# A two-layer mLSTM and RG-LRU trunk on one core: in-projections moved from channel-major to token-major

## The chip, the cores and the metric

The kernel runs on one core of a Trainium2 chip. The metric is the device time of one execution in microseconds. One execution was also taken with the hardware profiler; its trace gives the rows shown below. TensorE does the matmuls (PE, with its weight loads as PEld), VectorE is DVE, ScalarE is ACT, GpSimd is POOL, and SP only issues DMAs.

## The reference

The trunk takes x of 256 tokens by 2048 channels through two layers. All is float32. Cut to what matters, a layer is:

```python
u = rms_norm(x, norm_g)
p = u @ w_in                                    # 2048 x 12304
qk, v, o, z_a, ig, fg, xb, z_b = split(p)       # 2048 columns each, ig and fg 8 each
q, k = split(silu(causal_dwconv(qk, qk_conv)))  # 4 taps along the tokens
h = mlstm(q, k, v, i_pre, log_f) * sigmoid(o)   # 8 heads: q, k of 128, v of 256
y_a = head_norm(h) * head_norm_g * silu(z_a)
xc = causal_dwconv(xb, lru_conv_w) + lru_conv_b
y_b = rg_lru(xc, w_a, b_a, w_x, b_x, lam) * silu(z_b)   # gates: 8 blocks of 256x256
x = x + concat(y_a, y_b) @ w_out                # 4096 x 2048
```

After the second layer comes a last `rms_norm` with `final_g`.

## The kernel before

Each layer runs in four groups g of two heads, which is 512 columns of every part of `w_in`. A group's work is a list of items: the in-projection chunks `o`, `v`, `qk`, `xb`, `z`, `zb` of 512 columns each, the gate matmuls (`gate`), and four chunks of the out-projection of the group before (`out`, the fill). `_sequence` (L35) writes this order out by hand. In group 0 of a layer it is o, v, qk, xb, z, gate; in group 1 it is o, zb of group 0, v, qk, two fills, xb, two fills, z, gate, zb; later groups are the same without the zb of group 0. The last group of the first layer is followed by its out-projection in the order of units 0, 2, 1, 3; the last group of the second by `last_out` (L814), whose first eight halves need only `ya` and whose other eight need `yb`.

Weights come as units of 128 x 2048 floats (1 MB), loaded by SP into three buffers `raw` (L230) and used in two halves. `prepare` (L248) makes a half ready three halves ahead (`AHEAD`): ScalarE rounds it to `wH` (L261), VectorE subtracts to get the rest `wL` (L262, in the trace at the helper's L151). There are four buffers of each. Every product is taken in three parts (high by high, high by low, low by high), since the matmul's operand type holds fewer bits than float32.

Two matmul loops exist. `mm_a` (L266, token-major) holds 128 tokens of x as the stationary operand and streams 512 weight columns: for each of 16 row tiles and 2 token tiles three matmuls of 512 columns, 96 in a chunk; the result has tokens on the partitions. `mm_b` (L282, channel-major) holds 128 weight columns and streams tokens: for `wH` one matmul of 512 columns (high and low part of x side by side), for `wL` one of 256 columns, 128 matmuls in a chunk; the result has channels on the partitions. Before the change qk, xb and zb use `mm_b` in two parts `s_` of 256 channels, because the convolutions and the recurrence run along the tokens within a partition; o, v, z and the out-projection use `mm_a`.

A channel-major result is evacuated by `evac_b` (L363): a copy on ScalarE, an addition and a product on VectorE; the product with `rb` puts in the norm's factor for each token. For the convolutions it goes into a padded tile (`evac_pad`, L370), and `conv` (L353) takes one ScalarE operation and three VectorE operations for each tile of 128 channels.

What follows a chunk is a Python generator in a queue `bg`. After each half, `pump` (L202) lets the first generators in the queue emit instructions until a budget (`credit`) is used up: 1.05 for at most two generators, else 2.6. `require(key)` runs the first generators until something is there, for instance `xc` before the gate matmuls (`gate_before`) or `ybT` before the second unit of an out chunk. The engines' instruction streams come from a scheduler that orders instructions by readiness and by their place in the program.

Of the kernel before, what the change touches and what calls it, by code (L numbers as in the profile page):

```python
# [16 lines left out]
P = 128  # L17
# [10 lines left out]
AHEAD = 3  # L28

# [41 lines left out]

@with_exitstack
def tile_trunk(ctx, tc, x, xt, par, gw, gb, ws, final_g, out):
# [11 lines left out]
    st = {"nload": 0, "credit": 0.0, "pair": 0, "aux": 0}  # L85
# [42 lines left out]
    def load_x(c):  # L128
# [6 lines left out]
        nc.sync.dma_start(out=st["xa"][:, :, cs], in_=xv[:, :, cs])  # L135
        square_sum(c)
# [65 lines left out]
    def pump(budget):  # L202
        st["credit"] = min(st["credit"] + budget, budget)
        while bg and st["credit"] > 0:
            try:
                c = next(bg[0])
            except StopIteration:
                bg.popleft()
# [3 lines left out]
            st["credit"] -= c  # L212
# [16 lines left out]
    def load_unit(n, item, j):  # L229
        raw = wraw.tile([P, 2048], F32, tag="raw", name="raw")  # L230
        st["nload"] += 1
        u = blocks[item, j]
        if n < 4:
            w = 512 if n == 0 else 1024
            for o in range(0, 2048, w):
                if o % 1024 == 0:
                    load_xt(n, o // 1024)
                nc.sync.dma_start(out=raw[:, o : o + w], in_=ws[u][:, o : o + w])
        else:
            nc.sync.dma_start(out=raw, in_=ws[u])  # L240
        return raw

    def add_unit(mms, before=None, after=None):
        box = {}
        halves.append([dict(box=box, i=i, mm=mms[i], split=None,
                            before=before if i == 0 else None, after=after if i == 1 else None) for i in range(2)])

    def prepare(hf):  # L248
        n = len(xT_parts) if hf["i"] == 0 else 1
        if hf["i"] == 0:  # L250
            hf["box"]["raw"] = load_unit(n, *hf["at"])
            if n < 4:
                split_xT(0, n, xT_parts[n], range(4 * n, 4 * n + 4))
            if 4 <= st["nload"] < 8:
                load_x(st["nload"] - 4)
        r = hf["box"]["raw"][:, 1024 * hf["i"] : 1024 * hf["i"] + 1024]
        H = wsp.tile([P, 1024], F32R, tag="H", name="wH")
        L = wsp.tile([P, 1024], F32R, tag="L", name="wL")
        w = 1024 if n else 512
        for o in range(0, 1024, w):  # L260
            S.copy(out=H[:, o : o + w], in_=r[:, o : o + w])  # L261
            tt_(L[:, o : o + w], r[:, o : o + w], H.bitcast(F32)[:, o : o + w], ALU.subtract)  # L262
        hf["split"] = (H, L)


    def mm_a(acc, aH, aL, k0, first, last):  # L266
        def f(H, L):
            Hv = H.rearrange("p (k c) -> p k c", k=2)
            Lv = L.rearrange("p (k c) -> p k c", k=2)
            a_H, a_L, ps = aH(), aL(), acc()  # L270
            for k in range(2):
                kt = k0 + k
                for t in range(2):
# [3 lines left out]
                    PE.matmul(ps[:, t, :], a_H[:, kt, tsl], Hv[:, k, :], start=s, stop=False)  # L277
                    PE.matmul(ps[:, t, :], a_H[:, kt, tsl], Lv[:, k, :], start=False, stop=False)  # L278
                    PE.matmul(ps[:, t, :], a_L[:, kt, tsl], Hv[:, k, :], start=False, stop=e)  # L279
# [17 lines left out]
    def chunk_in(l, kind, g, postfn, beforefn=None):  # L297
# [9 lines left out]
        if kind in ("qk", "xb", "zb"):  # L307
# [5 lines left out]
        else:  # L313
            acc = make_acc()
            for u in range(4):
                mms = [mm_a(acc, lambda: st["x"][:, :, 0], lambda: st["x"][:, :, 1], 4 * u + 2 * i,
                            u == 0 and i == 0, u == 3 and i == 1) for i in range(2)]
                add_unit(mms, before=beforefn if u == 0 else None,
                         after=(lambda: postfn(acc())) if u == 3 else None)
# [33 lines left out]
    def conv(padt, o, ct, wcol, l, bias, oc=None):  # L353
        oc = ct if oc is None else oc
        wv = pars[:, l, wcol : wcol + 4]
        if bias is None:
            S.activation(out=o[:, oc, :], in_=padt[:, ct, 0:T], func=AF.Copy, scale=wv[:, 0:1])
        else:
            S.activation(out=o[:, oc, :], in_=padt[:, ct, 0:T], func=AF.Identity, scale=wv[:, 0:1], bias=bias)
        for j in range(1, 4):  # L360
            stt(o[:, oc, :], padt[:, ct, j : j + T], wv[:, j : j + 1], o[:, oc, :], ALU.mult, ALU.add)
# [7 lines left out]

    def evac_pad(l, acc):  # L370
        padt = work.tile([P, 2, 260], F32, tag="pad", name="padt", bufs=2)
        G.memset(padt[:, :, 0:3], 0.0)
        evac_b(l, padt[:, :, 3 : 3 + T], acc)
        return padt
# [112 lines left out]
    def v_post(l, g, acc):  # L487
# [11 lines left out]
        st["v", l, g] = (vH, vL)  # L499
        bg.append(e_gen(l, g))  # L500

    def qk_post(l, g, acc, h):
        padt = evac_pad(l, acc)

        def gen():
            qc = work.tile([P, 2, T], F32, tag="c4", name="qc", bufs=2)
            sg = work.tile([P, 2, T], F32, tag="sC", name="qsg")
            for ct in range(2):
                conv(padt, qc, ct, O_QKW + 4 * (8 * ct + 2 * g + h), l, None)
# [3 lines left out]
            yield 0.6  # L513
            q = work.tile([P, 2, 2, T], F32R, tag="xcs", name="qks")
            S.copy(out=q[:, :, 0, :], in_=qc)
            tt_(q[:, :, 1, :], qc, q.bitcast(F32)[:, :, 0, :], ALU.subtract)
            yield 0.6
            yield None
            yield None
            yield None  # L520
            yield None
            E, em, so, (vH, vL) = st["E", l, g], st["em", l], st["so", l, g], st["v", l, g]
            ps = aux("ps_S")
            for o_, ss_, ts__ in ((0, slice(0, 128), slice(0, 256)), (256, slice(128, 256), slice(128, 256))):
                mm3(ps[:, o_ : o_ + ts__.stop - ts__.start], q[:, 1, 0, ss_], q[:, 1, 1, ss_],
                    q[:, 0, 0, ts__], q[:, 0, 1, ts__])
            Pt = work.tile([P, 384], F32, tag="Pt", name="Pt")
            stt(Pt, ps[:, 0:384], DK_SCALE, E[:, h, :], ALU.mult, ALU.mult)
            PH = work.tile([P, 384], F32R, tag="sD", name="PH")
            PL = work.tile([P, 384], F32R, tag="sC", name="PL")  # L530
# [3 lines left out]
            yield None  # L534
            yield None
            yield None
            if h == 0:
                st["hh", l, g] = work.tile([P, 2, 2, 256], F32, tag="sE", name="hh")
                st["mv", l, g] = small.tile([P, 2, 2, 2], F32, tag="mv", name="mv", bufs=1)
            hh, mv = st["hh", l, g], st["mv", l, g]  # L540
            for t in range(2):
                pn = aux("ps_n")
                o = pn[:, 0:258]
                a = slice(P * t, P * t + P)
                mm3(o, PH[:, a], PL[:, a], vH[:, 0, h, :], vL[:, 0, h, :], last=t == 0)
                if t == 1:
                    mm3(o, PH[:, 256:384], PL[:, 256:384], vH[:, 1, h, :], vL[:, 1, h, :], first=False)
                dn = small.tile([P, 1], F32, tag="dn", name="dn")
                stt(dn, pn[:, 256:257], -1.0, em[:, t, 2 * g + h : 2 * g + h + 1], ALU.mult, ALU.max)
                tt_(dn, dn, pn[:, 256:257], ALU.max)  # L550
                V.reciprocal(out=dn, in_=dn)
                stt(hh[:, t, h, :], pn[:, 0:256], dn, so[:, t, 256 * h : 256 * h + 256], ALU.mult, ALU.mult)
                bs = small.tile([P, 6], F32, tag="bs", name="bs")
                V.bn_stats(out=bs, in_=hh[:, t, h, :])
                V.bn_aggr(out=mv[:, t, h, :], in_=bs)
                yield 1.1
            if h == 0:
                return
# [49 lines left out]
    def xb_post(l, g, acc, s_):  # L608
        padt = evac_pad(l, acc)

        def gen():
            if s_ == 0:
                st["xcf", l, g] = work.tile([P, 4, T], F32, tag="c4", name="xc", bufs=2)
                st["xcs", l, g] = work.tile([P, 4, 2, T], F32R, tag="xcs", name="xcs")
            xc, xs = st["xcf", l, g], st["xcs", l, g]
            for ct in range(2):
                tix = 4 * g + 2 * s_ + ct
                conv(padt, xc, ct, O_LW + 4 * tix, l, pars[:, l, O_LB + tix : O_LB + tix + 1], oc=2 * s_ + ct)
                yield 1.2
            sl_ = slice(2 * s_, 2 * s_ + 2)  # L620
            S.copy(out=xs[:, sl_, 0, :], in_=xc[:, sl_, :])
            tt_(xs[:, sl_, 1, :], xc[:, sl_, :], xs.bitcast(F32)[:, sl_, 0, :], ALU.subtract)
            if s_ == 1:
                st["xc", l, g] = (xc, xs)
            yield 0.6
# [66 lines left out]
    def zb_post(l, g, acc, s_):  # L692
# [96 lines left out]
    def emit_in(l, kind, g):  # L789
# [17 lines left out]
        posts = {"o": o_post, "v": v_post, "qk": qk_post, "xb": xb_post, "z": z_post, "zb": zb_post}  # L807
# [111 lines left out]
    for n, hf in enumerate(order_):  # L919
        while nprep < len(order_) and nprep <= n + AHEAD:  # L920
# [104 lines left out]
```

## Time and profile before

| | |
|---|---|
| median of 3 runs | 1523.73 us (1523.44 to 1524.4) |
| the profiled execution | 1523.95 us, span from first to last instruction 1521.9 us |
| granted TensorE clock, mean | 0.998 |
| busy: PE, PEld, DVE, ACT, POOL | 1504.0, 1285.5, 1079.2, 890.5, 62.3 us |
| DMA | 309.02 MB, mean 203 GB/s |
| matmuls and weight loads | 7704 each |

The rows have the form: line, engine, operation, written tile `<-` read tiles, shape, count, then busy time and mean duration in ns, then the idle time of the engine ahead of them and what ended it. Busy times overlap: a matmul counts as busy from its start to the modelled end of its pipeline, so a row's mean duration is longer than the distance from one matmul to the next. The waits table gives who waited for whom: us in total, times, longest. A list by time gives start, duration and what ran. A row for a stretch of time gives the stretch, its length, and the busy time and count of PE, PEld, DVE, ACT and POOL, then the granted clock, the DMA share and GB/s.

### The profile page before, as it was taken

The page shows a single profiled execution, that of the slowest core. Times are in us where ns is not written, and L with a number is a line of the kernel's source. Part 1 is how long each engine was busy: PE and PEld are TensorE (multiplying, and loading weights), DVE is VectorE, ACT ScalarE, POOL GpSimd, SP SyncE. Part 2 cuts the span into 40 slices and gives each one's busy share as a digit, 9 for nine tenths or more (in the row PEclk, how much of TensorE's full clock was granted, in tenths as well). Part 3 has the DMA queues.
Part 4 walks back from the last instruction along what each step waited for, and adds up shares of the span by engine and source line. Part 5 has one row for each costly group of instructions (what it writes and reads, how often), then busy time and mean ns, then how long its engine had stood idle before and what let it go on. Part 6 is the DMA issues. An engine that isn't in the chain of part 4 may idle for free.

```text
span 1521.9 us, 19969 instructions
## 1 busy us (share of the span) xinstructions
PE 1504.0 (99%) x7704; PEld 1285.5 (84%) x7704; DVE 1079.2 (71%) x1510; ACT 890.5 (59%) x1151; POOL 62.3 (4%) x136
## 2 busy tenths in 40 slices
PE   8999999999999999999999999999999999999997
PEld 6888888888888888888888888888888888888885
DVE  6887866676776857758658886775857759477584
ACT  6667655574555745548655585554845557455574
POOL 0010100000000000000001010000000000000002
PEclk9999999999999999999999999999999999999999
DMA  9654556745576555775655545566555675566762
GB/s 351 242 189 173 202 198 200 224 173 197 190 220 204 187 190 194 240 232 192 222 193 181 193 173 194 193 206 217 193 194 180 207 221 190 186 203 223 245 207 102
DMA packets 52927, 309.02 MB, mean 203 GB/s; under 512 B 5713, under 2 KB 8289, under 8 KB 19553
## 3 DMA queue, kind: packets, MB, share of 16 engines
q1 hardware_dynamic: 45776, 287.59, 52.3%
q0 software_dynamic: 4448, 15.75, 5.9%
q10 hardware_dynamic: 2608, 4.42, 0.8%
q8 instruction: 60, 0.98, 0.3%
q14 instruction: 35, 0.28, 0.1%
HBM read 288.85 MB, written 18.89 MB: 202 GB/s over the span
## 4 chain that ended last, share of the span: by engine, by line
PE 98%; DMA 1%; ACT 1%; DVE 0%; issue 0%; ACTq 0%
PE acc L292 35%; PE acc L277 18%; PE acc L279 18%; PE acc L278 18%; PE ps_gt L642 3%; PE acc L843 0%; PE acc L844 0%; PE acc L845 0%; PE ps_ty L596 0%; PE acc_x L844 0%; PE acc_x L843 0%; PE acc_x L845 0%; DMA raw<-in_ws_dram 0%; PE ps_n L473 0%; PE ps_n L475 0%; PE ps_n L474 0%
## 5 line engine op out<-in xcount | busy, mean ns | idle before, releaser
L151 DVE TENSOR_TENSOR wL<-raw,wH 128x1024 fp32r<-128x1024 f32 (+1 forms) x529 | 642.3, 1220 | 341.0 <-ACT wH L261 340.3
L261 ACT CAST wH<-raw 128x1024 fp32r<-128x1024 f32 (+1 forms) x529 | 552.3, 1048 | 469.8 <-PE acc L279 252.1
L292 PE MATMUL acc<-x_s,wH 128*128 128x512 f32 x1536 | 385.2, 393 | 0.0
L292 PEld LDWEIGHTS acc<-x_s,wH 128*128 128x128 f32 x1536 | 277.1, 189 | 50.4
L277 PE MATMUL acc<-wH,x_s 128*128 128x512 f32 x768 | 300.5, 391 | 6.6 <-ACT wH L261 6.6
L278 PE MATMUL acc<-wL,x_s 128*128 128x512 f32 x768 | 299.8, 390 | 0.8 <-DVE wL L151 0.8
L279 PE MATMUL acc<-wH,x_s 128*128 128x512 f32 x768 | 299.5, 390 | 0.0
L292 PEld LDWEIGHTS acc<-x_s,wL 128*128 128x128 f32 x1536 | 209.5, 190 | 15.0
L292 PE MATMUL acc<-x_s,wL 128*128 128x256 f32 x1536 | 214.1, 282 | 0.0
L277 PEld LDWEIGHTS acc<-wH,x_s 128*128 128x128 f32 x768 | 144.6, 188 | 36.5 <-ACT wH L261 6.9
L278 PEld LDWEIGHTS acc<-wL,x_s 128*128 128x128 f32 x768 | 144.6, 188 | 30.9 <-DVE wL L151 1.5
L279 PEld LDWEIGHTS acc<-wH,x_s 128*128 128x128 f32 x768 | 144.5, 188 | 30.0
L277 PE MATMUL acc<-wH,ybH 128*128 128x512 f32 x224 | 88.0, 393 | 0.0
L277 PE MATMUL acc<-wH,yaH 128*128 128x512 f32 x224 | 87.4, 390 | 0.0
L279 PE MATMUL acc<-wH,ybL 128*128 128x512 f32 x224 | 87.4, 390 | 0.0
L278 PE MATMUL acc<-wL,yaH 128*128 128x512 f32 x224 | 87.3, 390 | 0.0
L278 PE MATMUL acc<-wL,ybH 128*128 128x512 f32 x224 | 87.2, 389 | 0.0
L279 PE MATMUL acc<-wH,yaL 128*128 128x512 f32 x224 | 87.2, 389 | 0.0
L279 PEld LDWEIGHTS acc<-wH,ybL 128*128 128x128 f32 x224 | 42.0, 188 | 9.0
L279 PEld LDWEIGHTS acc<-wH,yaL 128*128 128x128 f32 x224 | 42.1, 188 | 8.8
L277 PEld LDWEIGHTS acc<-wH,yaH 128*128 128x128 f32 x224 | 42.1, 188 | 8.3
L278 PEld LDWEIGHTS acc<-wL,yaH 128*128 128x128 f32 x224 | 42.1, 188 | 8.2
(189 smaller groups left out, 1434.3 us busy)
## 6 DMA issues: line engine op xcount, KB each, us to landing
raw<-in_ws_dram SPq DMA_DIRECT2D x260, 1024.0 KB, 4.8
x_d<-stage POOLq DMA_DIRECT2D x24, 512.0 KB, 5.4
x_d<-x_acc ACTq DMA_DIRECT2D x8, 512.0 KB, 8.5
x_acc<-x_d SPq DMA_DIRECT2D x8, 512.0 KB, 4.7
raw<-in_ws_dram SPq DMA_DIRECT2D x6, 512.0 KB, 7.7
xp<-in_xt_dram SPq DMA_DIRECT2D x8, 256.0 KB, 7.2
x_acc<-in_x_dram SPq DMA_DIRECT2D x4, 512.0 KB, 9.9
nb<-nG_d POOLq DMA_DIRECT2D x8, 256.0 KB, 4.0
```

The lines of the kernel that those rows point to most:

```text
L151: return V.tensor_tensor(out=o, in0=a, in1=b, op=op)
L261: S.copy(out=H[:, o : o + w], in_=r[:, o : o + w])
L277: PE.matmul(ps[:, t, :], a_H[:, kt, tsl], Hv[:, k, :], start=s, stop=False)
L278: PE.matmul(ps[:, t, :], a_H[:, kt, tsl], Lv[:, k, :], start=False, stop=False)
L279: PE.matmul(ps[:, t, :], a_L[:, kt, tsl], Hv[:, k, :], start=False, stop=e)
L292: PE.matmul(ps[:, ct, T * part : 2 * T], W[:, k, P * ct : P * ct + P], moving, start=first and k == 0 and part == 0, stop=last and k == 3 ...
L642: PE.matmul(o, W[:, ib, jl], xs[:, ib, a, :], start=j == 0 and i == 0 and W is Hv and a == 0, stop=i == 1 and W is Lv, skip_group_check=True)
```

## The change

All chunks of qk, xb and zb become token-major except zb of group 3 in layer 0. The weight units stay in DRAM as they are; the load of a converted unit takes halves of two stored units (two DMAs of 512 KB), so that a half holds, for two row tiles, 256 columns of part 0 and 256 of part 1, lying 512 elements apart. A matmul streams both runs as one operand of 512 columns (`paired`).

The token-major result then has to become channel-major. `to_channels` copies it with the norm's factor to `tok` (ScalarE, in runs of 32), transposes all 32x32 blocks in one VectorE instruction to `blk`, writes `blk` to a DRAM tile `moved` with four DMAs on SP, and reads that into `fr` with one DMA on POOL. The generator then passes its turn in four pumps (`LANDING`), joins `fr` to `ch` with one ScalarE copy (qk and xb; zb reads `fr` directly) and goes on as before, now for four tiles of 128 channels at once. A pass (`"wait"`) lets the next generators in the queue go on. `conv` reads without padding, `qks` gets a tag of its own (`qs`), and the loads of raw units and of x are issued ahead of `prepare`. In group 0 qk now comes ahead of v.

```diff
+LANDING = 4
...
-            items = [("in", l, "o", g)] + ([("in", l, "zb", 0)] if g == 1 else []) + [("in", l, "v", g)]
             fill = [("out", l, g - 1, c) for c in range(4)] if g > 0 else []
-            items += [("in", l, "qk", g)] + fill[0:2] + [("in", l, "xb", g)] + fill[2:4]
+            head = {0: ("o", "qk", "v"), 1: ("o", "zb", "v", "qk")}.get(g, ("o", "v", "qk"))
+            items = [("in", l, k, 0 if k == "zb" else g) for k in head]
+            items += fill[0:2] + [("in", l, "xb", g)] + fill[2:4]
...
+def _by_channel(l, kind, g):
+    return (l, kind, g) == (0, "zb", NG - 1)
...
     def pump(budget):
...
-        while bg and st["credit"] > 0:
+        i = 0
+        while i < len(bg) and st["credit"] > 0:
             try:
-                c = next(bg[0])
+                c = next(bg[i])
...
+            if c == "wait":
+                i += 1
+            else:
+                st["credit"] -= c
...
+        elif hf["paired"]:
+            o = 1024 * (j % 2)
+            for s_ in range(2):
+                u = blocks[item, 2 * s_ + j // 2]
+                nc.sync.dma_start(out=raw[:, 1024 * s_ : 1024 * s_ + 1024], in_=ws[u][:, o : o + 1024])
...
+    def mm_a(acc, aH, aL, k0, first, last, paired=False):
         def f(H, L):
+            cols = "p (s k c) -> p k s c" if paired else "p (k c) -> p k c"
+            Hv = H.rearrange(cols, k=2, **({"s": 2} if paired else {}))
...
+                    o = ps[:, t, :].rearrange("p (s c) -> p s c", s=2) if paired else ps[:, t, :]
+                    PE.matmul(o, a_H[:, kt, tsl], Hv[:, k], start=s, stop=False)
+                    PE.matmul(o, a_H[:, kt, tsl], Lv[:, k], start=False, stop=False)
+                    PE.matmul(o, a_L[:, kt, tsl], Hv[:, k], start=False, stop=e)
...
+    def to_channels(l, acc):
+        require(("rstd", l))
+        rstd = st["rstd", l]
+        tok = work.tile([P, 4, 4, 2, 32], F32, tag="tok", name="tok")
+        blk = work.tile([P, 4, 256], F32, tag="blk", name="blk")
+        fr = work.tile([P, 4, 4, 2, 32], F32, tag="fr", name="fr", bufs=2)
+        for t in range(2):
+            S.activation(out=tok[:, :, :, t, :].rearrange("p m c j -> p c m j"),
+                         in_=acc[:, t, :].rearrange("p (c m j) -> p c m j", c=4, m=4), func=AF.Copy,
+                         scale=rstd[:, t : t + 1])
+        V.transpose(out=blk.rearrange("p m n -> p (m n)"), in_=tok.rearrange("p m c t j -> p (m c t j)"))
+        moved = dram.tile([P, 4, 256], F32, tag="moved", name="moved", bufs=2)
+        for a in range(4):
+            nc.sync.dma_start(out=moved[:, a].rearrange("(m j) n -> j m n", m=4), in_=blk[32 * a : 32 * a + 32])
+        G.dma_start(out=fr.rearrange("p a c t i -> p a (c t i)"), in_=moved)
+        return fr
...
+    def joined(fr):
+        ch = work.tile([P, 4, T], F32, tag="ch", name="ch")
+        S.copy(out=whole(ch), in_=pieces(fr))
+        return ch
...
+    def xb_post(l, g, acc):
+        fr = to_channels(l, acc)
         def gen():
+            for _ in range(LANDING):
+                yield "wait"
+            ch = joined(fr)
+            yield 0.3
+            xc = work.tile([P, 4, T], F32, tag="c4", name="xc", bufs=2)
+            xs = work.tile([P, 4, 2, T], F32R, tag="xcs", name="xcs")
+            for ct in range(4):
+                tix = 4 * g + ct
+                conv(ch, xc, ct, O_LW + 4 * tix, l, pars[:, l, O_LB + tix : O_LB + tix + 1])
                 yield 1.2
...
+    def zb_post(l, g, acc):
+        fr = to_channels(l, acc)
+        def gen():
+            for _ in range(LANDING):
+                yield "wait"
+            while ("lru", l, g) not in st or ("yT", l, g) not in st and g > 0:
+                yield "wait"
...
+            S.activation(out=whole(sg), in_=pieces(fr), func=AF.Sigmoid)
+            tt_(whole(zb), whole(sg), pieces(fr), ALU.mult)
...
         while nprep < len(order_) and nprep <= n + AHEAD:
+            while st["nload"] < len(order_) // 2 and st["nload"] <= (nprep + 5) // 2:
+                load_unit(order_[2 * st["nload"]])
             prepare(order_[nprep])
```

`qk_post` changes in the same way as `xb_post`: one generator for both heads instead of one for each, with the waits between its steps as `"wait"`.

More of the change, by code (lines that the diff above doesn't have):

```diff
@@ L244, in add_unit @@
+        if 3 <= n < 7:
+            load_x(n - 3)
+    def add_unit(mms, before=None, after=None, paired=False):
         box = {}
-        halves.append([dict(box=box, i=i, mm=mms[i], split=None,
+        halves.append([dict(box=box, i=i, mm=mms[i], split=None, paired=paired,
                             before=before if i == 0 else None, after=after if i == 1 else None) for i in range(2)])
     def prepare(hf):
-        n = len(xT_parts) if hf["i"] == 0 else 1
+        n = st["nprep"]
         if hf["i"] == 0:
-            hf["box"]["raw"] = load_unit(n, *hf["at"])
@@ L263, in prepare @@
-        hf["split"] = (H, L)
-    def mm_a(acc, aH, aL, k0, first, last):
+            if 3 <= n < 7:
+                use_x(n - 3)
+        else:
+            st["nprep"] += 1
+        raw = hf["box"]["raw"]
+        if hf["paired"]:
+            r = raw.rearrange("p (s n) -> p s n", s=2)[:, :, 512 * hf["i"] : 512 * hf["i"] + 512]
+        else:
+            r = raw.rearrange("p (i n) -> p i n", i=4)[:, 2 * hf["i"] : 2 * hf["i"] + 2, :]
+        H = wsp.tile([P, 2, 512], F32R, tag="H", name="wH")
@@ L316, in chunk_in @@
                 mms = [mm_a(acc, lambda: st["x"][:, :, 0], lambda: st["x"][:, :, 1], 4 * u + 2 * i,
-                            u == 0 and i == 0, u == 3 and i == 1) for i in range(2)]
+                            u == 0 and i == 0, u == 3 and i == 1, paired) for i in range(2)]
                 add_unit(mms, before=beforefn if u == 0 else None,
-                         after=(lambda: postfn(acc())) if u == 3 else None)
+                         after=(lambda: postfn(acc())) if u == 3 else None, paired=paired)
     def bc(ap2, n):
@@ L533, in gen @@
             yield 1.0
[L534 to L556, printed above, removed]
@@ L606, in z_post @@
         bg.append(gen())
-    def xb_post(l, g, acc, s_):
-        padt = evac_pad(l, acc)
+    def xb_post(l, g, acc):
+        fr = to_channels(l, acc)
         def gen():
[L612 to L618, printed above, removed]
-                yield 1.2
[L620 to L625, printed above, removed]
+            for _ in range(LANDING):
+                yield "wait"
+            ch = joined(fr)
+            yield 0.3
+            xc = work.tile([P, 4, T], F32, tag="c4", name="xc", bufs=2)
+            xs = work.tile([P, 4, 2, T], F32R, tag="xcs", name="xcs")
+            for ct in range(4):
+                tix = 4 * g + ct
+                conv(ch, xc, ct, O_LW + 4 * tix, l, pars[:, l, O_LB + tix : O_LB + tix + 1])
+                yield 1.2
+            for b in range(2):
+                sl_ = slice(2 * b, 2 * b + 2)
+                S.copy(out=xs[:, sl_, 0, :], in_=xc[:, sl_, :])
+                tt_(xs[:, sl_, 1, :], xc[:, sl_, :], xs.bitcast(F32)[:, sl_, 0, :], ALU.subtract)
+                yield 0.6
+            st["xc", l, g] = (xc, xs)
         bg.append(gen())
```

149 lines of the change are left out of this document (89 added, 60 removed).

## The prediction

> **What bounds the kernel now.** I read the busy shares first, then the waits of TensorE, then the chain that ended last, and last the pitch (start to start) of single matmuls.
>
> ```profile
> span 1521.9 us, 19969 instructions
> PE 1504.0 (99%) x7704; PEld 1285.5 (84%) x7704; DVE 1079.2 (71%) x1510; ACT 890.5 (59%) x1151; POOL 62.3 (4%) x136
> PEclk9999999999999999999999999999999999999999
> PE acc L277 <- ACT wH L261: 6.6, 1, 6.6
> PE acc L278 <- DVE wL L151: 0.8, 1, 0.8
> PE 98%; DMA 1%; ACT 1%; DVE 0%; issue 0%; ACTq 0%
> ...
> 156.85 22.32 PE acc L292 x128
> ...
> 200.96 22.32 PE acc L292 x128
> ...
> 299.67 0.39 PE L278 MATMUL acc<-wL,x_s 128*128 128x512 f32 x1
> ...
> 312.36 0.39 PE L277 MATMUL acc<-wH,x_s 128*128 128x512 f32 x1
> ```
>
> TensorE waits twice in the whole run, 7.4 us in all, both at the start; it carries 98% of the chain and holds its full clock. So the time is the number of matmuls times their pitch, and every other engine is hidden as long as it keeps up. Matmuls overlap, so the 390 ns of one is no price. The prices are these: a channel-major chunk (L292) is one piece of 128 matmuls, 64 of 512 and 64 of 256 columns, 22.32 us. In the token-major loop (L277 to L279) the 57 starts from 299.67 to 312.36 give 12.69 / 56 = 0.2266 us a matmul. A token-major chunk has 96 of them, all of 512 columns: 96 x 0.2266 = 21.75 us, and one half unit (12 matmuls) is 2.72 us. Both kinds stream 49,152 columns; 32 fewer matmuls make the difference of 0.57 us.
>
> **The change, part by part.** *Matmuls.* Of the 24 chunks of kinds qk, xb and zb, 23 turn token-major: 23 x 0.57 = 13.1 us less on the path, if a paired matmul keeps the pitch. Its moving operand is two runs of 256 columns, 512 elements apart. No row shows such an operand, so I bound it: from below by 0.2266 (a contiguous operand of the same length), from above by two 256-column matmuls, each 22.32 / 64 - 0.2266 = 0.122 us, together 0.244 us; then a chunk is 23.4 us and the 23 cost 25 us more than now. I take 0.2266, because columns, weights and the written PSUM range are the same; below it nothing is to be had, as the operand streams no faster in pieces.
>
> The Trainium skill, "TensorE: Matmul & The Clock Gate", section "Wait — 56ns, not 53.3ns?", puts the fixed cost of a warm matmul at about 2.5 ns, 215.7 ns for 512 columns; by it 32 fewer matmuls would save 0.08 us a chunk, 1.8 us in all. The trace has 226.6 ns for that shape and both chunks as measured pieces, so the trace's difference decides.
>
> *Evacuation on ScalarE and VectorE.* A channel-major chunk was evacuated by two copies on ScalarE and four operations on VectorE; now by two scaled copies, one transpose and, for qk and xb, one joining copy.
>
> ```profile
> L365 ACT COPY padt<-acc 128x512 f32<-128x512 f32 x32 | 18.7, 583 | 0.0
> L151 DVE TENSOR_TENSOR padt<-padt,acc 128x512 f32<-128x512 f32 x32 | 21.7, 678 | 0.0
> L151 DVE TENSOR_TENSOR padt<-padt,rb 128x512 f32<-128x512 f32 x32 | 22.2, 694 | 1.0
> L577 ACT ACTIVATE sz<-acc,rstd 128x512 f32<-128x512 f32 x16 | 11.0, 690 | 7.0 <-PE ps_n L475 3.1 <-PE acc L279 2.2 <-DVE za L154 1.7
> L678 ACT ACTIVATE gate<-gate 128x1024 f32<-128x1024 f32 x8 | 8.5, 1064 | 0.1
> L151 DVE TENSOR_TENSOR wL<-raw,wH 128x1024 fp32r<-128x1024 f32 x527 | 640.9, 1222 | 338.4 <-ACT wH L261 337.7
> L159 DVE TENSOR_SCALAR Dt<-Dt 128x1024 f32<-128x1024 f32 x8 | 5.5, 692 | 2.5 <-ACT Dt L659 2.5
> L154 DVE SCALAR_TENSOR_TENSOR qc<-padt,pars,qc 128x256 f32<-128x256 f32 x96 | 42.2, 479 | 4.4 <-ACT qc L357 3.8
> ```
>
> VectorE loses 2 x (0.68 + 0.69) = 2.74 us and gains one 32x32 transpose of 128x1024, not in the trace; the rows of that size lie between 0.69 and 1.22, and I take 1.22: about 1.5 us less a chunk, 35 us of 1079. ScalarE loses 1.17 and gains 2 x 0.69 + 1.06: 1.3 us more, some 25 us of 890. Neither ends a wait of TensorE, so both are priced at nothing; the merged two-head attention and 4-tile operations move less. The padding memsets on POOL go, which nobody on the path awaits.
>
> *The way through DRAM.* Four writes of 128 KB on SP, one read of 512 KB on POOL.
>
> ```profile
> raw<-in_ws_dram SPq DMA_DIRECT2D x260, 1024.0 KB, 4.8
> x_d<-stage POOLq DMA_DIRECT2D x24, 512.0 KB, 5.4
> x_d<-x_acc ACTq DMA_DIRECT2D x8, 512.0 KB, 8.5
> x_acc<-x_d SPq DMA_DIRECT2D x8, 512.0 KB, 4.7
> nb<-nG_d POOLq DMA_DIRECT2D x8, 256.0 KB, 4.0
> out_dram<-x_acc SPq DMA_DIRECT2D x8, 256.0 KB, 3.0
> SPq L240 <- DVE wL L151: 1188.0, 230, 14.0
> DMA packets 52927, 309.02 MB, mean 203 GB/s; under 512 B 5713, under 2 KB 8289, under 8 KB 19553
> ```
>
> From the chunk's last matmul to the data in `fr`: evacuation 1.4; transpose 0.7 to 1.2, behind another VectorE operation 0 to 1.2; writes 3.0 (the output store) to 8.5 (the x store); read 4.0 (nb) to 5.4 (x_d). That is 9.1 to 17.7 us. I take 1.4 + 1.2 + 0.6 + 3.9 (between 3.0 and 4.7) + 5.4 = 12.5 us.
>
> Queued behind a late `fr` is ScalarE, in order: the joining copy, then the cast of the next weights. How long may ScalarE stand?
>
> ```profile
> 301.00 1.05 ACT L261 CAST wH<-raw 128x1024 fp32r<-128x1024 f32 x1 [1.67 <-PE acc L279]
> 303.72 1.05 ACT L261 CAST wH<-raw 128x1024 fp32r<-128x1024 f32 x1 [1.67 <-PE acc L279]
> ```
>
> A cast starts when TensorE has finished a half and freed its H buffer (2.72 us apart), and serves the half that starts three halves, 8.2 us, later. The join is issued after four waits, so after the cast that starts 8.2 us behind the chunk's end. The next cast's half starts at 7 x 2.72 = 19.0; ahead of it lie join 1.06, cast 1.05 and subtraction 1.22, so `fr` may land at 15.7. If the instruction order puts the join one cast earlier, at 13.0. With 12.5 both hold: nothing on the path. The zb chunks read `fr` in their sigmoid, with the same place in the queue.
>
> On SP the writes wait for the transpose, and weight loads stand behind them. SP already waits most of the run for raw buffers (1188 us), and three buffers turn over in 6 x 2.72 = 16.3 us; one is in use about 5.2 (two casts 2.72 apart, the second with its subtraction), a load takes 4.8, some 6 us remain. The wait for `blk` (about 3 us behind the chunk's end) fits, as does a paired load in two DMAs of 512 KB. On POOL the read stands ahead of nb and the masks; POOL is 4% busy. DRAM traffic grows by 23 x 1 MB on 309 MB. All of it at nothing.
>
> *Order of the work.* In group 0, xb is followed by z (8 halves, 21.8 us) and the gates, which need all four convolved tiles.
>
> ```profile
> 129.39 0.28 PE L474 MATMUL ps_n<-vL,PH 128*128 128x258 f32 x1
> 129.51 0.28 PE L642 MATMUL ps_gt<-xcs,wH 128*128 128x256 f32 x1
> 129.63 0.40 PE L475 MATMUL ps_n<-vH,PL 128*128 128x258 f32 x2
> 127.00:140.00 13.00, 12.93 (x84) 11.53 (x84) 10.73 (x30) 10.13 (x19) 0.55 (x1) 1.00 0.30 114
> ```
>
> The gate matmuls already run between those of the attention here, so TensorE takes what is ready, and it is busy 12.93 of 13.00 us: no gain is left (at most 0.07 us). After the change: 12.5 + join 1.06 + on VectorE 12 x 0.48 + 2 x 0.68 = 7.1 us beside a 1.22 us subtraction every 2.72, so 7.1 / 0.55 = 12.9: ready at 26.5, against 21.8 plus two prepared halves of the next chunk (5.4) = 27.2. With nothing run ahead TensorE would stand 4.7 us; with the late `fr` and two halves ahead 4.5. I take 1.5 us, nearer to none, twice (two layers): 3 us. Elsewhere xb has two output chunks and z ahead of it, 43 us.
>
> At the end, zb of layer 1 feeds the last stage:
>
> ```profile
> 1467.79 0.40 PE L843 MATMUL acc<-wH,yaH 128*128 128x512 f32 x1
> 1478.75 0.68 DVE L151 TENSOR_TENSOR ybL<-zb,ybH 128x512 fp32r<-128x512 f32 x1
> 1489.58 0.39 PE L843 MATMUL acc<-wH,ybH 128*128 128x512 f32 x1
> ```
>
> zb ends at 1467.8, yb is ready 11.6 us later and first used 21.8 us later. After: 12.5 + sigmoid 1.06 + two products 2.44 + split 1.3 = 17.3, with two subtractions between 19.7: still in time, 0 taken; with `fr` at 17.7 it is 3.1 us late. zb of layer 0 has only four halves there and is not converted.
>
> **Sum**, against the profiled execution, 1523.95 us (span 1521.9; median of the runs 1523.73): 1523.95 - 13.1 + 3 = 1513.9 us, 0.65% less; I say 1514. About 0.2%, 3 us, is what a measurement of this kernel can tell from no change.
>
> **Rivals.** *The data return too late, and the time is longer than before.* If `fr` lands d us behind its due time (13.0 or 15.7), ScalarE holds back the casts and TensorE stands d us in each of 23 chunks. The gain is gone at d = 10.1 / 23 = 0.44 us. With 17.7 against 15.7, d = 2.0: 1513.9 + 46 = 1560; with 14.5 against 13.0, 1548; a typical miss of 1 us gives 1537. For it: the 8.5 us of the x stores and the in-order queues. Against: the other DMA rows sum to 12.5. Chance 0.16.
>
> *The paired operand streams as two short ones.* 1523.95 + 25 + 3 = 1552. For it: no row has such an operand. Against: equal columns. Chance 0.05. The Trainium skill, "Advanced Engine Details and Errata", section "PSUM Cachelines", says that any access pattern that isn't contiguous slows matmuls significantly; no run here shows one.
>
> *The gain is eaten in the few tight places.* Both gate stages at 4.7 and the end at 3.1: 1523.95 - 13.1 + 12.5 = 1523.4, no change. For it: VectorE's 10.73 of 13 us in that window. Chance 0.09.
>
> **How the numbers follow.** The forecast has 0.70 (its own range 1510 to 1519: all 13.1 saved and nothing lost, to both gate stages at 4.7). Faster 0.70; same 0.09; slower 0.16 + 0.05 = 0.21. The range goes from 1509.5 to 1537, the typical late return; the costlier half of that rival and the slow operand, some 0.13, stay outside, and a little below.
>
> **What would show it.** Right: single 21.75 us stretches of the token-major line for qk, xb and zb; TensorE's wait table still nearly empty; `fr` landing by 13 us behind the chunk's end. Wrong: a pitch above 0.23 us in paired matmuls; TensorE waiting for `wH` or `wL` some 19 us after each converted chunk, with ScalarE waiting for the DMA into `fr`; holes ahead of `ps_gt` in group 0 or ahead of `ybH` at the end.

## The result, and the profile after

The changed kernel takes 1514.65 us (median of 4 runs, 1514.13 to 1515.24), the kernel before 1523.71 us beside it (1523.44 to 1524.4): a ratio of 0.994, 95% interval 0.9923 to 0.9957, so 9.1 us less. The profiled execution took 1515.08 us. Forecast were 1514 us, in a range of 1509.5 to 1537.

Span, busy times, the chain that ended last and TensorE's waits of the changed kernel:

```profile
span 1513.4 us, 18528 instructions
PE 1492.8 (99%) x6968; PEld 1246.5 (82%) x6968; DVE 1040.6 (69%) x1404; ACT 907.2 (60%) x1139; POOL 66.7 (4%) x127
PE 94%; DVE 3%; DMA 1%; ACT 1%; issue 1%; SPq 0%; ACTq 0%; DVEq 0%
PE acc L303 <- ACT wH L286: 6.4, 1, 6.4
PE acc L304 <- DVE wL L160: 3.1, 3, 1.6
```

There are 736 matmuls fewer, 23 x 32. TensorE is still the bound, but 3% of the chain now runs through VectorE. TensorE waits for a `wL` three times instead of once, 3.1 us instead of 0.8; what else it lost stands between matmuls and in no row of waits. VectorE lost 38.6 us of work and ScalarE gained 16.7.

First and last matmul, by time, of a stretch of a converted chunk (qk, layer 1):

```profile
967.75 0.39 PE L303 MATMUL acc<-wH,x_s 128*128 128x512 f32 x1
...
971.60 0.39 PE L305 MATMUL acc<-wH,x_s 128*128 128x512 f32 x1
```

That is 18 matmuls, (971.60 - 967.75) / 17 = 0.2265 us apart: the paired operand keeps the pitch that the plain operand has before. So 23 x 0.57 = 13.1 us are there to be had, and the span fell by 8.5. I went through all distances between starts of matmuls and added up what the ones over 0.3 us exceed 0.227: 4.9 us before, 9.9 after. About 1 us of the 5 more is ahead of 20 us, in the start, and 4 us in group 0 of the two layers. (The start holds 2.2 to 3.9 us of such excess in the traces of the changed kernel and of the experiments and 3.0 in the kernel before, so the 1 us may not come from the change at all.) Of group 0, the two stretches from the first attention to the gates (length, then busy time of PE, PEld, DVE, ACT, POOL, granted clock, DMA share and GB/s), of before and then after:

```profile
85.00:135.00 50.00, 49.93 (x281) 43.46 (x280) 41.66 (x78) 28.82 (x39) 3.04 (x8) 1.00 0.53 195
840.00:885.00 45.00, 44.93 (x244) 38.72 (x243) 35.33 (x65) 21.89 (x28) 0.31 (x3) 1.00 0.52 183
```

```profile
85.00:135.00 50.00, 49.82 (x246) 41.49 (x245) 42.64 (x77) 34.02 (x39) 7.93 (x12) 1.00 0.64 221
840.00:885.00 45.00, 43.42 (x212) 35.97 (x211) 35.35 (x67) 30.76 (x36) 2.22 (x7) 1.00 0.62 215
```

and the largest hole of the second, by time:

```profile
879.13 0.40 PE L303 MATMUL acc<-wH,x_s 128*128 128x512 f32 x1
881.08 0.50 PE L304 MATMUL acc<-wL,x_s 128*128 128x512 f32 x1 [1.56 <-DVE wL L160]
```

PE is idle 1.58 us of 45 where before it was idle 0.07. The hole is a subtraction of weights that came late, on an engine that is busy with convolutions, attention and gates at that time. The stretch around it, before and then after, shows VectorE (the third pair) going from 6.79 to 11.00 of 11.00 us:

```profile
873.00:884.00 11.00, 10.93 (x61) 9.23 (x60) 6.79 (x15) 5.29 (x7) 0.00 (x0) 1.00 0.55 202
873.00:884.00 11.00, 9.42 (x50) 7.42 (x49) 11.00 (x36) 7.30 (x9) 0.10 (x1) 1.00 0.46 147
```

The way through DRAM, as one chunk of qk went it: ScalarE from the chunk's end on, then the transpose, the issue of the four writes and of the read, and the rows for all chunks.

```profile
972.03 1.27 ACT L398 ACTIVATE tok<-acc,rstd 128x512 f32<-128x512 f32 x2 [1.67 <-PE acc L305]
973.19 1.05 ACT L286 CAST wH<-raw 128x1024 fp32r<-128x1024 f32 x1
...
985.63 1.05 ACT L286 CAST wH<-raw 128x1024 fp32r<-128x1024 f32 x1 [0.76 <-PE acc L305]
986.59 1.04 ACT L416 COPY ch<-fr 128x1024 f32<-128x1024 f32 x1
973.33 1.25 DVE L401 STREAM_TRANSPOSE blk<-tok 128x1024 f32<-128x1024 f32 x1 [1.71 <-ACT tok L398]
974.60 1.79 SPq L404 DMA_DIRECT2D moved<-blk  x4
979.54 0.53 POOL L405 DMA_DIRECT2D fr<-moved  x1 [43.01 <-DMA moved<-blk]
moved<-blk SPq DMA_DIRECT2D x92, 128.0 KB, 2.3
fr<-moved POOLq DMA_DIRECT2D x23, 512.0 KB, 6.3
L398 ACT ACTIVATE tok<-acc,rstd 128x512 f32<-128x512 f32 x46 | 29.1, 685 | 38.2 <-PE acc L305 38.2
L401 DVE STREAM_TRANSPOSE blk<-tok 128x1024 f32<-128x1024 f32 x23 | 28.7, 1246 | 19.0 <-ACT tok L398 18.8
L416 ACT COPY ch<-fr 128x1024 f32<-128x1024 f32 x16 | 16.7, 1046 | 2.4 <-DMA fr<-moved 2.4
```

The chunk's last matmul is the one at 971.60 above and ends at 972.0. Evacuation and transpose end 2.6 us later, the read is issued 7.5 us later, and `fr` is there at 986.4, 14.4 us behind the chunk's end. Over all 23 chunks it is 10.5 to 16.9 us, 14.0 in the median. (The expectations below say 13.7: they count from the end of the first of the two evacuating copies, up to 0.7 us later.) Between the evacuation and the join ScalarE issues six casts (four of them and a copy of the out-projection are left out here), and the join comes when ScalarE reaches it. The last row is the verdict on the way through DRAM: 16 joins waited 2.4 us for `fr` in the whole run.

### The profile page after: what moved, and what is told of

Its sections match the earlier page's. It is cut to its first block, busy times and chain, and to the rows that moved or that the text cites. A ratio compares the mean times of both kernels' runs of the same rounds, so it can differ in the third digit from the quotient of the medians.

```text
span 1513.4 us, 18528 instructions
## 1 busy us (share of the span) xinstructions
PE 1492.8 (99%) x6968; PEld 1246.5 (82%) x6968; DVE 1040.6 (69%) x1404; ACT 907.2 (60%) x1139; POOL 66.7 (4%) x127
## 4 chain that ended last, share of the span: by engine, by line
PE 94%; DVE 3%; DMA 1%; ACT 1%; issue 1%; SPq 0%; ACTq 0%; DVEq 0%
PE acc L304 28%; PE acc L305 28%; PE acc L303 28%; PE ps_gt L696 3%; PE acc L318 1%; DVE wL L160 1%; DVE xc L163 1%; PE acc L925 0%; PE acc L927 0%; PE acc L926 0%; DMA xp<-in_xt_dram 0%; PE acc_x L927 0%; PE acc_x L925 0%; PE acc_x L926 0%; PE ps_ty L648 0%
## 5 line engine op out<-in xcount | busy, mean ns | idle before, releaser
L303 PE MATMUL acc<-wH,x_s 128*128 128x512 f32 x1504 | 587.5, 391 | 6.4 <-ACT wH L286 6.4
L304 PE MATMUL acc<-wL,x_s 128*128 128x512 f32 x1504 | 586.8, 390 | 3.2 <-DVE wL L160 3.1
L305 PE MATMUL acc<-wH,x_s 128*128 128x512 f32 x1504 | 585.9, 390 | 0.0
L303 PEld LDWEIGHTS acc<-wH,x_s 128*128 128x128 f32 x1504 | 282.7, 188 | 65.3 <-ACT wH L286 7.0
L304 PEld LDWEIGHTS acc<-wL,x_s 128*128 128x128 f32 x1504 | 282.6, 188 | 63.9 <-DVE wL L160 6.4
L305 PEld LDWEIGHTS acc<-wH,x_s 128*128 128x128 f32 x1504 | 282.6, 188 | 58.3
L398 ACT ACTIVATE tok<-acc,rstd 128x512 f32<-128x512 f32 x46 | 29.1, 685 | 38.2 <-PE acc L305 38.2
L304 PEld LDWEIGHTS acc<-wL,ybH 128*128 128x128 f32 x224 | 42.1, 188 | 8.3
L303 PEld LDWEIGHTS acc<-wH,ybH 128*128 128x128 f32 x224 | 42.1, 188 | 8.3
L829 ACT COPY stage<-acc 128x1024 f32<-128x1024 f32 x24 | 24.4, 1017 | 38.5 <-PE acc L305 38.5
```

The costliest lines, as they stand in the source:

```text
L303: PE.matmul(o, a_H[:, kt, tsl], Hv[:, k], start=s, stop=False)
L304: PE.matmul(o, a_H[:, kt, tsl], Lv[:, k], start=False, stop=False)
L305: PE.matmul(o, a_L[:, kt, tsl], Hv[:, k], start=False, stop=e)
L398: S.activation(out=tok[:, :, :, t, :].rearrange("p m c j -> p c m j"), in_=acc[:, t, :].rearrange("p (c m j) -> p c m j", c=4, m=4), func= ...
L829: S.copy(out=stage, in_=ps)
```

## The experiments

All times below are medians. The kernel before took 1523.59 us beside four of these kernels (zb taken back, one run, xb ahead of v, the join held early) and 1523.31 us beside the other four.

**Back to channel-major, in part.** zb alone is taken back, seven chunks more than the one.

```diff
 def _by_channel(l, kind, g):
-    return (l, kind, g) == (0, "zb", NG - 1)
+    return kind == "zb"
```

> Seven more chunks (all of zb) go back to channel-major, 16 stay token-major. Theory (the time is the matmul count times the pitch, 0.56 us a chunk by the pieces of 22.32 and 96 x 0.2267): 7 x 0.56 = 3.9 us more than the changed kernel's 1514.65, that is 1518.6. First rival (the saving comes from the new order, the earlier loads and the tag of its own, not from the matmuls): 1514.7, no change. Second rival (the way through DRAM costs about as much as it saves where the result is needed soon, as with zb): at or below 1514.7.

Measured: 1519.06 us (1518.07 to 1520.26), ratio 0.997 (0.9959 to 0.9982). That is 4.4 us more than the changed kernel, 0.63 us a chunk where the pitch says 0.57; the runs of each kernel spread by 1 to 2 us, so the two agree. The gain scales with the number of converted chunks and has the size of the 32 matmuls.

**One run instead of two.** The weight units of qk, xb and zb lie in DRAM in token-major order, so that a load is one DMA of 1 MB and the operand one run of 512.

```diff
-        paired = kind in ("qk", "xb", "zb")
+        paired = False
...
+            for u in range(4):
+                units.append([("w_in", l, (sl(512 * u + 256 * i, 256), cs)) for i in range(2)])
```

> The converted chunks' weights are stored in DRAM in the order in which the token-major matmul streams them: one load of 1 MB for a unit instead of two of 512 KB, and a moving operand of one run of 512 columns instead of two runs of 256. Theory (the two-run operand streams at the same pitch, 0.2267 us, and the split loads are hidden): 1514.6, within 1 us. Rival (two runs or split loads cost something): each ns a matmul is worth 23 x 96 = 2.2 us, so a two-run pitch 1 to 2 ns longer, or late loads, would make this kernel 2 to 5 us faster, 1510 to 1512.

Measured: 1516.13 us (1514.02 to 1516.28), ratio 0.9947 (0.9935 to 0.996). Its loads of the units, apart from those at the start, are all alike:

```profile
raw<-in_ws_dram SPq DMA_DIRECT2D x260, 1024.0 KB, 4.9
```

No gain: neither the operand in two runs nor the 512 KB loads cost anything that can be measured. This is the second witness against the slow operand, beside the pitch. The rule of the Trainium skill that the prediction weighed there ("Advanced Engine Details and Errata", section "PSUM Cachelines": a non-contiguous pattern slows matmuls) isn't borne out for a moving operand of two runs of 256 elements: 0.2265 us with the runs, 0.2266 without. That section is about PSUM, and the written PSUM range is the same here.

**Group 0 in another order.** xb goes ahead of v, so that v and z, 43.5 us, lie between xb and the gates, where z alone (21.8) lay.

```diff
-            head = {0: ("o", "qk", "v"), 1: ("o", "zb", "v", "qk")}.get(g, ("o", "v", "qk"))
+            head = {0: ("o", "qk"), 1: ("o", "zb", "v", "qk")}.get(g, ("o", "v", "qk"))
...
-            items += [("in", l, "z", g), ("gate", l, g)] + ([("in", l, "zb", g)] if g > 0 else [])
+            items += ([("in", l, "v", g)] if g == 0 else []) + [("in", l, "z", g), ("gate", l, g)] + ([("in", l, "zb", g)] if g > 0 else [])
```

> In group 0 of both layers the order is o, qk, xb, v, z, gate: the convolved xb is wanted 16 halves (43 us) behind its chunk, not 8 (21.8 us). The changed kernel's matmul starts have about 4 us of holes in group 0 of the two layers that the kernel before has not. Theory (the data's return plus the convolutions on VectorE do not fit into 21.8 us, and VectorE, which is 100% busy there, holds back the weights' subtraction): the holes ahead of the gates go, 2 to 4 us less, 1511 to 1512.5. Rival (VectorE has that much work in group 0 in any order): the holes move, 1514.6.

Measured: 1510.84 us (1510.19 to 1512.14), ratio 0.9916 (0.9903 to 0.993), faster than both kernels. The same two stretches, and TensorE's waits:

```profile
85.00:135.00 50.00, 50.00 (x259) 42.73 (x258) 42.95 (x77) 33.80 (x42) 2.92 (x9) 1.00 0.61 220
840.00:885.00 45.00, 45.00 (x237) 38.76 (x236) 37.78 (x72) 32.15 (x43) 1.67 (x6) 1.00 0.54 203
PE acc L304 <- DVE wL L160: 0.6, 1, 0.6
```

TensorE is busy without a gap in both. In the stretch of the largest hole VectorE has time to spare again:

```profile
873.00:884.00 11.00, 11.00 (x80) 10.30 (x79) 8.15 (x26) 9.41 (x14) 0.10 (x1) 1.00 0.33 118
```

A full VectorE alone makes no hole: in this kernel it is busy 10.95 of 11.00 us from 851 to 862, and TensorE 11.00. What stands ahead of the subtraction must count too, but no run takes that by itself. The edit moves v and with it the attention too, so it shows that the order decides, and not which of the two moves does. The kernel lies 12.75 us under the one before, and 13.1 were to be had: the part of the saving that was missing had gone to group 0, and nowhere else of size. The earlier loads and the tag `qs` were not tried alone; beside 12.75 of 13.1 us they have little room.

**The old order of the head.** In group 0 v goes ahead of qk again, as in the kernel before.

```diff
-            head = {0: ("o", "qk", "v"), 1: ("o", "zb", "v", "qk")}.get(g, ("o", "v", "qk"))
+            head = {0: ("o", "v", "qk"), 1: ("o", "zb", "v", "qk")}.get(g, ("o", "v", "qk"))
```

> In group 0 of both layers v comes ahead of qk again, as in the kernel before; all else as changed. Theory (group 0 has too little time between the last converted chunk and the gates, and VectorE is full there): the attention of the two heads now starts 21.8 us later and falls together with the convolutions of xb, so the holes ahead of the gates grow, 2 to 8 us more than 1514.65. Rival (the order in group 0 is indifferent, holes only move): 1514.7.

Measured: 1517.1 us (1516.45 to 1518.3), ratio 0.996 (0.9948 to 0.9973), 2.45 us more than the changed kernel. Matmuls by time in layer 0:

```profile
124.28 0.50 PE L303 MATMUL acc<-wH,x_s 128*128 128x512 f32 x1 [0.38 <-ACT wH L286]
126.22 0.57 PE L304 MATMUL acc<-wL,x_s 128*128 128x512 f32 x1 [1.44 <-DVE wL L160]
126.59 0.63 PE L305 MATMUL acc<-wH,x_s 128*128 128x512 f32 x1
127.02 0.63 PE L303 MATMUL acc<-wH,x_s 128*128 128x512 f32 x1
```

After the distance of 1.94 us the next starts lie 0.43 us apart, not 0.227, up to 129.58; the granted clock is 0.50 from 126.5 to 129.9. Moving qk ahead of v, which the change does along with the rest, is thus worth as much as four converted chunks (4 x 0.57 = 2.3 us).

**No passes.** The generator doesn't give up its turn after the read.

```diff
-LANDING = 4
+LANDING = 0
```

> The four passes ahead of the join are left out (LANDING 0). The prediction's reading (the passes set the join's place in ScalarE's stream): the join stands right behind the evacuation, each cast behind it waits for the data, and the time rises by tens of us, above 1560. Theory after the traces (the stream is ordered by readiness, and the join stays behind six casts): within 1.5 us of 1514.65.

Measured: 1514.69 us (1514.07 to 1515.45), ratio 0.9944 (0.993 to 0.9957). No difference to the changed kernel: the join stands behind six casts here too. The passes don't put it there. That the scheduler's order by readiness does is what is left; no run shows it by itself.

**The join held early.** To find where the late return starts to cost, the join is put right behind the reads, and the third to sixth cast after it may not go ahead of it.

```diff
-            S.copy(out=H[:, o], in_=r[:, o])
+            cast = S.copy(out=H[:, o], in_=r[:, o])
+            if st.get("join") is not None:
+                st["since"] += 1
+                if 3 <= st["since"] <= 6:
+                    order(cast, st["join"])
...
-        S.copy(out=whole(ch), in_=pieces(fr))
+        st["join"], st["since"] = S.copy(out=whole(ch), in_=pieces(fr)), 0
...
-        fr = to_channels(l, acc)
+        ch = joined(to_channels(l, acc))
```

> The joining copy of qk and xb (16 chunks) is held in ScalarE's stream behind the second cast after the evacuation, instead of behind the sixth, where the instruction order of the changed kernel has it. Theory (a late return costs nothing because the join stands behind six casts; the cast behind the join must start 3.3 us ahead of its half): the third cast's half starts 5 x 2.72 = 13.6 us after the chunk, so the data would have to be there at 10.3; they come at 13.7 on average, so TensorE stands about 3.4 us in each of 16 chunks: 54 us more, about 1569. Rival (the casts have more slack than that, or ScalarE catches up): 1515 to 1520.

Measured: 1547.73 us (1547.0 to 1548.99), ratio 1.0159 (1.0145 to 1.0172), 33 us more than the changed kernel. ScalarE and then TensorE behind a qk chunk that ends at 417.4, and the reads:

```profile
428.28 1.01 ACT L831 COPY stage<-acc 128x1024 f32<-128x1024 f32 x1 [7.10 <-PE acc L309]
429.19 1.05 ACT L420 COPY ch<-fr 128x1024 f32<-128x1024 f32 x1
430.57 0.39 PE L309 MATMUL acc<-wH,yaL 128*128 128x512 f32 x1
431.24 0.51 PE L307 MATMUL acc<-wH,yaH 128*128 128x512 f32 x1 [0.28 <-ACT wH L286]
432.50 0.50 PE L308 MATMUL acc<-wL,yaH 128*128 128x512 f32 x1 [0.75 <-DVE wL L160]
fr<-moved POOLq DMA_DIRECT2D x23, 512.0 KB, 4.2
```

The chain of the prediction's first rival is seen: join, cast, subtraction, hole. What ScalarE waits for ahead of it is not the data, though, but the end of the out chunk, for the copy `stage` (7.1 us); `fr` landed 0.03 us before the join, in the six qk chunks of groups 1 to 3 0.03 to 0.26 us before. Copy and data come at the same time there, so this run shows what a join at 11.8 us costs, and not what the data alone would. Each of these six chunks costs 0.66 + 1.26 - 2 x 0.23 = 1.5 us, and the six xb chunks next to nothing. Most of the rest is group 0: distances of 4.5 us at 133, 6.5 and 1.3 at 834 to 842, 4.5 at 903, and a granted clock of 0.50 behind them (from 137.1 to 143.8, from 836.8 to 847.0 and from 908.5 to 911.8). Matmul by matmul, 21.9 of the 33.9 us by which the span is longer are lost there. The size that I expected was too large, since the reads take 4.2 us here instead of 6.3 and `fr` is there 11.6 to 11.8 us behind those qk chunks. That the casts that are held back keep the weight loads back, and so leave the reads alone, fits this, but no run takes it by itself.

**A second hop.** The data take one more way through DRAM before they are read.

```diff
-        G.dma_start(out=fr.rearrange("p a c t i -> p a (c t i)"), in_=moved)
+        moved2 = dram.tile([P, 4, 256], F32, tag="moved2", name="moved2", bufs=2)
+        G.dma_start(out=moved2, in_=moved)
+        G.dma_start(out=fr.rearrange("p a c t i -> p a (c t i)"), in_=moved2)
```

> The way through DRAM gets a second hop: POOL copies `moved` to another DRAM tile before it reads that into `fr`, in all 23 chunks, some 5.5 us more a chunk, so the data come about 19 us behind the chunk and not 13.7. The prediction's step (the join may find its data at 15.7 us at the latest, then each chunk costs the rest): 3.3 us x 23 = 76 us more, about 1590. Theory after the traces (the instruction order puts the join behind as many casts as the order's own estimate of the return asks for, six in the changed kernel, seven here, so the data may come at 21 to 24 us): nothing in the chunks of groups 1 to 3; only the two places where the result is wanted soon pay, the gates of group 0 in both layers (up to 5.5 us each) and the last stage, where `yb` was ready only a little ahead (about 3 us): 1520 to 1529.

Measured: 1560.48 us (1552.83 to 1562.51), ratio 1.0234 (1.0212 to 1.0257). Neither number holds. Hop and read, the join's wait in the table of waits, and one chunk (it ends at 423.4):

```profile
moved<-moved POOLq DMA_DIRECT2D x23, 512.0 KB, 4.5
fr<-moved POOLq DMA_DIRECT2D x23, 512.0 KB, 8.9
ACT ch L418 <- DMA fr<-moved: 95.1, 16, 10.2
448.01 1.05 ACT L418 COPY ch<-fr 128x1024 f32<-128x1024 f32 x1 [7.20 <-DMA fr<-moved]
453.28 0.50 PE L304 MATMUL acc<-wL,x_s 128*128 128x512 f32 x1 [1.79 <-DVE wL L160]
```

`fr` comes 16.1 to 26.8 us behind the chunk, later than I had reckoned, because the read takes 8.9 us instead of 6.3. The join here stands behind seven casts. ScalarE waits 95.1 us for it in all, and most of that TensorE does not feel: qk chunks of groups 1 to 3 whose data come by 22.1 us leave no hole; at 22.5 and 22.9 there is a distance of 0.7 and 1.2 us, and this one, at 24.6, leaves 0.8 and 2.3 us between 450 and 455. Five of the six xb chunks of these groups, with data at 24.1 to 26.8 us, leave distances of 0.6 to 1.3 us as well, two to four each. What else is lost are the gates of group 0 (8 to 9 us between 130 and 145, 6 us between 902 and 911) and the end (4.6 us at 1521). The mean granted clock is 0.989 against 0.997. So the spare time of the way through DRAM is some 8 us beyond the 14.0 that it takes, in the groups after the first and with seven casts ahead of the join, and about none in group 0.

**All 24 chunks.** zb of group 3 in layer 0 is converted too.

```diff
 def _by_channel(l, kind, g):
-    return (l, kind, g) == (0, "zb", NG - 1)
+    return False
```

> zb of group 3 in layer 0 is converted too: all 24 chunks token-major. Its result is wanted four halves (10.9 us) behind the chunk. Theory: the data come at 13.7 us, then sigmoid 1.06, two products 2.45 and the first split 1.3, so `yb` is there at about 18.5 us and TensorE stands 6 to 8 us; less 0.56 us saved, 1520 to 1522. Rival (the order finds other matmuls for the gap, for instance the first out chunks' `ya` half, already ahead of it): 1514.

Measured: 1525.87 us (1522.54 to 1527.03), ratio 1.0013 (1.0004 to 1.0022). One more chunk costs 11 us. Matmuls by time at the end of layer 0, and the stretch after the hole:

```profile
721.02 0.39 PE L305 MATMUL acc<-wH,yaL 128*128 128x512 f32 x1
729.78 0.80 PE L303 MATMUL acc<-wH,ybH 128*128 128x512 f32 x1 [8.38 <-ACT ybH L766]
730.38 0.63 PE L304 MATMUL acc<-wL,ybH 128*128 128x512 f32 x1
730.80 0.63 PE L305 MATMUL acc<-wH,ybL 128*128 128x512 f32 x1
729.80:734.40 4.60, 4.60 (x11) 3.60 (x12) 1.26 (x2) 0.45 (x1) 0.00 (x0) 0.50 0.01 4
```

The four halves after that chunk are 10.9 us, and the data need longer: `fr` is there 15.0 us behind the chunk's end, and the first `ybH` 19.2. TensorE stands 8.4 us, then runs at a granted clock of 0.50, with starts 0.43 us apart, for a dozen matmuls: 12 x (0.43 - 0.227) = 2.4 us more. Together 10.8 of the 11.2 us; a second slow stretch in this kernel is shown in the last section. The exception in the diff is what keeps the gain.

## Why the prediction was right, and where it wasn't

*Matmuls: right.* 0.57 us a chunk at an unchanged pitch; 0.63 measured by taking back seven chunks, and 12.75 us of 13.1 seen with the order of group 0 mended. The step that decided the forecast was to take the trace's difference for the price. By the fixed cost of 2.5 ns a matmul that the Trainium skill states ("TensorE: Matmul & The Clock Gate", section "Wait — 56ns, not 53.3ns?") the whole change would have brought an estimated 1.8 us; the result disagrees.

*Evacuation: right in sum, not everywhere free.* The transpose takes 1.246 us, taken were 1.22; VectorE has 38.6 us less for 35 forecast, ScalarE 16.7 more for 25. Both were priced at nothing on the ground that neither ends a wait of TensorE. In group 0 that doesn't hold: there a late subtraction on VectorE ends the largest hole, 1.56 us.

*The way through DRAM: 1.5 us short, inside the bounds.* For 12.5 us it is 14.0 in the median. Evacuation and transpose take 2.1 to 2.6 us (taken 3.2); the four writes, until the read is issued, 4.3 to 5.1 in 17 of the 23 chunks and 5.9 to 10.1 in the others (taken 3.9: each lands in 2.3 us, but SP issues them over 1.79); the read 6.3 (taken 5.4).

*The join's due time: wrong, on the safe side.* The prediction read "issued after four waits, so after the cast that starts 8.2 us behind the chunk's end" and made 15.7 us of it. The join stands behind the cast that starts 13.6 us behind; the next cast, at 16.3, serves the half that starts at 16.3 + 8.2 = 24.5, and `fr` is due at 24.5 - 3.3 = 21.2. Without the passes nothing changes, so they were the wrong witness. The prediction saw 3.2 us of spare, 12.5 against 15.7; against 21.2 the measured 14.0 leaves 7.2. So the step came out well by some luck: the data came later than taken, and a due time that was later still made up for it. Two chunks have their data 16.4 and 16.9 us behind their end, later than 15.7, and TensorE shows no hole in the 40 us behind either. This is why the late return didn't come. Its price, d for each of 23 chunks, was too high as well: with the join held early the xb chunks of groups 1 to 3 cost next to nothing. That a join which holds the casts back costs more than the whole gain is shown by both delayed kernels.

*Order of the work: the place right, the size nearly.* 3 us were taken for the gates of group 0. Some 4 us are there, as holes ahead of and among the gate matmuls and in the attention before; the bound of 4.7 a layer wasn't reached. The rest of the difference, about 1 us, lies in the start, which the prediction didn't look at and which differs by as much between the experiments' traces. That it comes from the two DMAs of a load is not shown: the kernel with single loads isn't faster.

*The end: the order right, the spare used up.* By time, around the last matmuls of zb and the first with `yb`:

```profile
1459.34 0.39 PE L925 MATMUL acc<-wH,yaH 128*128 128x512 f32 x1
...
1475.51 1.06 ACT L759 ACTIVATE zsg<-fr 128x1024 f32<-128x1024 f32 x1
...
1480.13 1.14 ACT L766 CAST ybH<-zb 128x512 fp32r<-128x512 f32 x2 [0.49 <-DVE zb L160]
...
1481.10 0.39 PE L925 MATMUL acc<-wH,ybH 128*128 128x512 f32 x1
```

The first matmul with `ybH` starts 1481.10 - 1459.34 = 21.8 us after zb, just when it is due, while the second of the two casts still runs (they take 1480.13 to 1481.27). Predicted were 2.1 us of spare; the sigmoid started 16.0 us behind the chunk's end (1459.5), behind the casts, not at 12.5. A little later it would have cost, as the second hop shows.

*The rivals.* The late return and the slow operand fall by the runs above. The gain eaten in tight places is the one that did happen in part: 4 us of 13, all of it in group 0 and none at the end.

## What to carry to other kernels

When one engine carries the whole chain, price a rewrite by its instruction count times the measured start-to-start distance of the shape, and then look for the few stages where the new, longer way to the result has no other work beside it: there the gain is given back, and putting more work between producer and consumer (here 3.8 us by one change of order, which moved v as well) returns it. A copy that waits for a transfer is due when the work behind it in the same engine's stream is due, so find its place in the stream that runs, not in the program text. Convert all but the one chunk that has no cover: here one of 24 cost 11 us, more than the 9.1 that the 23 others brought.

## What the hardware showed beyond that

A stall of TensorE can cost more than its length, and the same stall does not always. When the largest hole of the changed kernel ends (1.56 us idle at 879) the clock stays at 1.00; in the kernel with all 24 chunks the same hole (1.57 us idle at 889) is followed by 0.50:

```profile
881.00:885.00 4.00, 3.92 (x23) 3.33 (x24) 3.96 (x10) 3.33 (x4) 0.00 (x0) 1.00 0.75 248
891.70:895.00 3.30, 3.30 (x10) 2.59 (x9) 3.26 (x9) 2.38 (x3) 0.00 (x0) 0.50 0.89 318
```

At 0.50 the starts of 512-column matmuls lie 0.43 us apart. The clock stayed there for 3.4 us in this case and with v ahead of qk (126.5 to 129.9), for 6.8 with the join held early (137.1 to 143.9), and for 10.2 around the 8.4 us of idle time with all 24 chunks (724.4 to 734.6). The Trainium skill, "TensorE: Matmul & The Clock Gate", section "What's actually happening", tells of such a halved clock after an idle window of about 3.4 us and of a window as long to come back. The traces agree in the halving and in the 3.4 us, of which 6.8 and 10.2 are two and three; but the idle time ahead of the two short cases, 1.8 and 1.6 us, was less than such a window.

The other thing is the read from DRAM: in the median the same 512 KB landed in 4.2 us in the kernel that holds the casts back, 6.3 us in the changed kernel (3.5 to 7.9), and 8.9 us after another hop.
